# A stick-breaking attention whose pairs of heads share one score tile, and whose sample part is scanned

## The chip, the cores and the metric

The kernel runs on one core of one Trainium2 chip. The metric is device time in microseconds (us) of one execution, the median over runs. Five engines work beside each other, each with its own list of instructions taken strictly in order: TensorE (PE in the profile; its weight loads are PEld), VectorE (DVE), ScalarE (ACT), GpSimd (POOL) and SyncE (SP, which here issues DMAs).

## The reference, cut to what matters

One step of a two-layer encoder runs for 256 prompt frames and 32 sample frames together (`T = 288` columns). Layer 0 mixes frames with two softmax attentions (A and B), layer 1 with a stick-breaking attention (C). Cross-attention into 256 memory tokens and a squared-ReLU MLP follow in both layers. Only C is touched here. It has 16 heads of 64 features:

```python
def stick_breaking_attend(q, k, v, q_pos, k_pos):
    z = jnp.einsum('bqhd,bkhd->bhqk', q, k) * (HEAD_DIM ** -0.5)
    before = k_pos[None, :] < q_pos[:, None]
    log_keep = jnp.where(before, jax.nn.log_sigmoid(-z), 0.0)
    tail = lax.cumsum(log_keep, axis=3, reverse=True) - log_keep
    w = jnp.where(before, jnp.exp(jax.nn.log_sigmoid(z) + tail), 0.0)
    return jnp.einsum('bhqk,bkhd->bqhd', w, v)
```

The prompt's 256 queries see the prompt's 256 keys. The 32 sample queries see 256 cached keys and their own 32. With sp = softplus(z), the weight is exp(z minus the sum of sp over all keys from this one up to the query).

## The kernel before, in words

Activations lie with features on partitions and frames in columns. Every weight matrix streams in chunks of 256 columns. `load_chunk` lets SP load a raw fp32 chunk; ACT (and at times DVE) then rounds it into `wh`, a 4-byte type named fp32r that TensorE reads in one pass, and DVE or POOL subtracts to make the rest `wl`. `gemm2` makes each product from three matmuls (L159 to L161: high by high, low by high, high by low) into two PSUM banks named `g`, from a pool of three. The three `g` lines are most of the program.

Layer 1's attention is one phase, written in the order `ORD_C`: memory split, then for four groups of four heads `q` (queries and keys, `project_qk`), `p` (values, `project_v`) and `a` (`attend_c`), then `K0` to `K3`, the memory keys for the cross-attention that follows, and the output projection. That order is only a priority: the tile framework schedules all instructions against its own timeline and writes one fixed list for each engine. So PE's list has attention matmuls in between the `g` matmuls.

In `attend_c` each group has two pairs of heads (`p` = 0, 1); a pair shares one block of 128 feature rows, 64 for each head. Before the change it works as follows.

- Queries. `project_qk` writes them twice, each copy with the other head's 64 rows set to zero (`qz[:, p, par, :]`, by the mask `m8`), so that all 128 rows can be contracted.
- Scores of a pair. Keys lie on partitions. Bank `za` holds keys 0 to 127 against all queries of both heads (512 columns), bank `zb` keys 128 to 255 against queries 128 to 255 (256 columns). Queries and keys are split into fp32r halves (`split_into`), and three matmuls make each product (L578, L579).
- Softplus. ACT takes Abs (two calls), Exp and Ln, DVE finishes with max and add (two calls) into `sp`; POOL zeroes what is not below the diagonal (`below_diag`, two calls); ACT and DVE split `sp` into `sph` and `spl`.
- The running sum along keys is three matmuls for each of the halves, against a triangle of -1 (`mtrir`) and a block of -1 (`monesr`), added into `za` and `zb` (L599 to L601).
- Weights `w`: two Exp on ACT, two `below_diag` on POOL. `pv_prompt` (L473) multiplies with the values into `za`, `put_prompt` (ACT, then DVE) reads that out.
- The sample's scores `zs` also have keys on partitions: six plain fp32 matmuls (L618, L621), softplus in two pieces, five plain fp32 matmuls for the running sum (L628 to L632), two Exp, one select, `pv_sample` (L483), `put_sample`.

PSUM in this phase: three `g` banks, one bank `ps_t` for transposes and norms, and four banks for `za`, `zb` and `zs`. Plain fp32 matmuls stand in the trace as two passes each, so counts of their rows are double.

Of the kernel before, what the change touches and what calls it, by code (L numbers as in the profile page):

```python
# [52 lines left out]
def body(ctx: ExitStack, tc: tile.TileContext, i: dict, o: dict):  # L53
# [27 lines left out]
    def phase(kind):  # L81
        if R.stack is not None:
            R.stack.close()
        R.stack = ExitStack()
        R.step, R.pool_every, R.dve_every = STEP[kind]
        R.c = int(kind == "c")
        R.ph = R.stack.enter_context(tc.tile_pool(name="ph_" + kind, bufs=1))
        R.s = R.stack.enter_context(tc.tile_pool(name="s_" + kind, bufs=4 if kind[0] == "c" else 2, space=PS))
        R.m, R.o = ps_t, R.s
# [175 lines left out]
    fbias = const.tile([8, 1], F32, name="fbias")  # L265
    nc.sync.dma_start(out=fbias, in_=i["fbias"])
    eye32 = const.tile([P, NS], F32, name="eye32")
    for a in range(4):
        r = slice(32 * a, 32 * a + 32)
        dve.tensor_copy(eye32[r, :], ident[r, r])  # L270
        dve.tensor_copy(smask[r, NP_:T], bmask[r, P + 32 * a:P + 32 * a + 32])

    mtrir = const.tile([P, P], F32R, name="mtrir")
    dve.tensor_copy(mtrir, mtri_)
    mtri = mtrir.bitcast(F32)
    monesr = const.tile([P, P], F32R, name="monesr")
    dve.tensor_copy(monesr, mones_)
    mones = monesr.bitcast(F32)
# [3 lines left out]
    dve.tensor_copy(bdr, bd)  # L282

    qg = const.tile([P, 2, 2], F32, name="qg")
    for a in range(2):
# [100 lines left out]
        rstd_of(ps[:, 0:T], T, 1.0 / 64, r)  # L386

    def project_qk(wname, cq, ck, xh, xl, rs, norm, ko, oidx, ws0=None):
        qz = R.ph.tile([P, 2, 2, T], F32, tag="qz", name="qz", bufs=QZB[R.c])
        kT = R.ph.tile([P, 2, T], F32, tag="kT", name="kT", bufs=KTB[R.c])  # L390
        for which, chunk in ((0, cq), (1, ck)):
            ws = load_chunk(i[wname][chunk]) if ws0 is None or which else ws0
            pss = gemm2(ws, xh, xl, pool=R.s if FIRST_S and ws0 is not None and not which else ps_g)
            for p in range(2):
                ps = pss[p]
                if norm is None:
                    if which == 0:
# [140 lines left out]
        put_sample(oh, ol, kt0, po)  # L538


    def softplus(zs, w, a):

        c0 = 0
        for z in zs:
            c1 = c0 + z.shape[1]
            act(a[:, c0:c1], z, AF.Abs)
            c0 = c1
        act(a, a, AF.Exp, scale=-1.0)
        act(a, a, AF.Ln, bias=1.0)
        c0 = 0  # L550
        for z in zs:
            c1 = c0 + z.shape[1]
            dve.scalar_tensor_tensor(w[:, c0:c1], z, 0.0, a[:, c0:c1], ALU.max, ALU.add)
            c0 = c1

    def below_diag(x, pattern):

        nc.gpsimd.affine_select(x, x, pattern=pattern, compare_op=ALU.is_gt, fill=0.0, base=0,
                                channel_multiplier=-1)

    def attend_c(g, qz, kT, vt, ck, cv, oh, ol):
        kt0 = 2 * g
        k_ = dict(start=False, skip_group_check=True)
        for p in range(2):

            za = bank(R.s, "za")
            zb = bank(R.s, "zb")
            za2 = za.rearrange("p (e q) -> p e q", e=2)
            if ZR:
                qh = R.ph.tile([P, 2, NP_], F32R, tag="qh", name="qh")  # L570
                ql = R.ph.tile([P, 2, NP_], F32R, tag="ql", name="ql")
                kh = R.ph.tile([P, NP_], F32R, tag="kh", name="kh")
                kl = R.ph.tile([P, NP_], F32R, tag="kl", name="kl")
                split_into(kh, kl, kT[:, p, 0:NP_])
                split_into(qh, ql, qz[:, p, :, 0:NP_])
                f_ = True
                for x, y in ((kh, qh), (kh, ql), (kl, qh)):
                    mm(za2, x[:, 0:P], y, start=f_, stop=False, skip_group_check=True)  # L578
                    mm(zb[:, 0:NP_], x[:, P:NP_], y[:, :, P:NP_], start=f_, stop=False, skip_group_check=True)  # L579
                    f_ = False  # L580
            else:
                mm(za2, kT[:, p, 0:P], qz[:, p, :, 0:NP_], start=True, stop=False, skip_group_check=True)
                mm(zb[:, 0:NP_], kT[:, p, P:NP_], qz[:, p, :, P:NP_], start=True, stop=False, skip_group_check=True)
            a = R.ph.tile([P, 768], F32, tag="a", name="a", bufs=2)
            sp = R.ph.tile([P, 768], F32, tag="pr", name="sp", bufs=4)
            softplus([za, zb[:, 0:NP_]], sp, a)
            dia = [[0, 2], [1, P]]
            below_diag(sp[:, 0:512].rearrange("p (e q) -> p e q", e=2)[:, :, 0:P], dia)
            below_diag(sp[:, 512:768].rearrange("p (e q) -> p e q", e=2), dia)
            sh = R.ph.tile([P, 768], F32R, tag="a", name="sph", bufs=2)  # L590
            if SHE:
                dve.tensor_copy(sh, sp)
            else:
                act(sh, sp, AF.Copy)
            sl = R.ph.tile([P, 768], F32R, tag="pr", name="spl", bufs=4)
            dve.tensor_tensor(sl, sp, sh.bitcast(F32), ALU.subtract)
            for x, end in ((sh, False), (sl, True)):
                xb = x[:, 512:768]
# [3 lines left out]
            w = R.ph.tile([P, 768], F32, tag="pr", name="w", bufs=4)  # L602
            act(w[:, 0:512], za, AF.Exp)
            act(w[:, 512:768], zb[:, 0:NP_], AF.Exp)
            below_diag(w[:, 0:512].rearrange("p (e q) -> p e q", e=2)[:, :, 0:P], dia)
            below_diag(w[:, 512:768].rearrange("p (e q) -> p e q", e=2), dia)
            po = za
            pv_prompt(po, p, vt, [(w[:, par * NP_:(par + 1) * NP_], w[:, 512 + par * P:512 + (par + 1) * P])
                                  for par in range(2)])
            put_prompt(oh, ol, kt0 + p, po)  # L610

        z = bank(R.s, "zs")
        fl = True
        for p in range(2):
            q = qz[:, p, :, NP_:T]
            for kk in range(2):
                c0 = kk * P + p * 64
                mm(z[:, c0:c0 + 64], ck[:, p, kk * P:(kk + 1) * P], q, start=fl, stop=False, skip_group_check=True)  # L618
                fl = False
            c0 = 2 * P + p * 64  # L620
            mm(z[0:NS, c0:c0 + 64], kT[:, p, NP_:T], q, start=False, stop=False, skip_group_check=True)  # L621
        a = R.ph.tile([P, 768], F32, tag="a", name="as_", bufs=2)
        sp = R.ph.tile([P, 768], F32, tag="pr", name="sps", bufs=4)
        softplus([z[:, 0:2 * P]], sp[:, 0:2 * P], a[:, 0:2 * P])
        softplus([z[0:NS, 2 * P:384]], sp[0:NS, 2 * P:384], a[0:NS, 2 * P:384])
        n3 = sp[0:NS, 2 * P:384]
        below_diag(n3, [[0, 4], [1, NS]])
        mm(z[:, 0:2 * P], mtri, sp[:, 0:2 * P], stop=False, **k_)  # L628
        mm(z[:, 0:P], mones, sp[:, P:2 * P], stop=False, **k_)
        for c0 in (0, P):  # L630
            mm(z[:, c0:c0 + P], mones[0:NS, :], n3, stop=False, **k_)
# [5 lines left out]
        act(w3, z[0:NS, 2 * P:384], AF.Exp)
# [379 lines left out]
```

## Time and profile before

| | us |
|---|---|
| median of 3 runs | 972.64 (972.23 to 972.69) |
| the profiled execution | 970.67 |
| its span, first to last instruction | 969.0 |
| PE busy in it | 955.4 |
| DVE, ACT, POOL busy | 681.5, 541.6, 249.2 |

Between 500 and 672 us lies layer 1's C phase with its memory keys and its output projection. Durations of one matmul in the profile include a tail that overlaps with the next, so the time that a matmul costs in a stream is read from the distance between starts.

### The profile page before, as it was taken

Reading aid. Unit: us, or ns where it says so; the run is one execution under the profiler, and the core shown is the slowest. Engines: PE = TensorE matmul, PEld = TensorE weight load, DVE = VectorE, ACT = ScalarE, POOL = GpSimd, SP = SyncE. Lnnn points to the kernel's source line nnn. Section 1 sums busy time; section 2 is a strip of 40 time slices with the busy share of each in tenths; the row PEclk is TensorE's granted clock in tenths of the full one; section 3 lists DMA queues with packets and bytes.
Section 4 is the critical chain, followed back from the end, with each engine's and each line's share of the span. In section 5 each row is a group of like instructions: output and inputs, shape, how many; then the busy total and the mean of one; then the engine's idle time right before and its main releaser. Section 6 shows DMA issues by size and latency. Waiting matters only on the chain.

```text
span 969.0 us, 19373 instructions
## 1 busy us (share of the span) xinstructions
PE 955.4 (99%) x7276; PEld 922.2 (95%) x7276; DVE 681.5 (70%) x1460; ACT 541.6 (56%) x1268; POOL 249.2 (26%) x291
## 2 busy tenths in 40 slices
PE   8999989999999999999999999999999999999998
PEld 8998878999999999999999999989999999999998
DVE  8788848879678767776695656778977766464643
ACT  6667647656456645444474677865554655454531
POOL 4311472221212211121122322323543112121110
PEclk8999998999999999999999999999999999999999
DMA  8654353754555555555566444356443455555452
GB/s 264 200 173 162 116 198 112 245 167 141 170 170 171 161 168 166 162 170 163 168 197 207 142 142 152 100 196 200 139 157 127 153 175 169 162 167 169 160 174 72
DMA packets 50702, 160.03 MB, mean 165 GB/s; under 512 B 6296, under 2 KB 12968, under 8 KB 50352
## 3 DMA queue, kind: packets, MB, share of 16 engines
q1 hardware_dynamic: 46864, 148.69, 47.9%
q0 software_dynamic: 2592, 8.92, 2.4%
q10 hardware_dynamic: 1152, 1.18, 0.4%
q8 instruction: 57, 0.93, 0.4%
q14 instruction: 37, 0.30, 0.1%
HBM read 148.65 MB, written 10.12 MB: 164 GB/s over the span
## 4 chain that ended last, share of the span: by engine, by line
PE 91%; DMA 3%; DVE 3%; issue 2%; POOL 1%; ACT 0%; SPq 0%; DVEq 0%; ACTq 0%; POOLq 0%
PE g L159 27%; PE g L161 27%; PE g L160 26%; DVE wl L145 1%; DMA raw<-in_w_kv_dram 1%; DMA bsmp<-cd 1%; PE za L473 1%; PE za L578 1%; DMA b<-cd 1%; PE zs L618 0%; PE s L516 0%; POOL b L844 0%; PE sx L159 0%; PE po L473 0%; PE za L599 0%
## 5 line engine op out<-in xcount | busy, mean ns | idle before, releaser
L144 ACT ACTIVATE wh<-raw 128x512 fp32r<-128x512 f32 (+3 forms) x561 | 279.8, 550 | 234.2 <-PE g L160 116.3
L145 DVE TENSOR_TENSOR wl<-raw,wh 128x512 fp32r<-128x512 f32 (+3 forms) x483 | 315.7, 687 | 113.7 <-ACT wh L144 107.5
L145 POOL TENSOR_TENSOR wl<-raw,wh 128x512 fp32r<-128x512 f32 (+2 forms) x141 | 175.0, 1241 | 530.8 <-ACT wh L144 430.7
L159 PE MATMUL g<-xh,wh 128*128 128x288 f32 (+1 forms) x1032 | 303.1, 298 | 1.1 <-ACT wh L144 0.7
L161 PE MATMUL g<-xh,wl 128*128 128x288 f32 (+1 forms) x1032 | 302.9, 298 | 1.3 <-DVE wl L145 1.2
L160 PE MATMUL g<-xl,wh 128*128 128x288 f32 (+1 forms) x1032 | 303.8, 297 | 0.0
L161 PEld LDWEIGHTS g<-xh,wl 128*128 128x128 f32 (+1 forms) x1032 | 193.0, 188 | 4.0 <-DVE wl L145 2.6
L159 PEld LDWEIGHTS g<-xh,wh 128*128 128x128 f32 (+1 forms) x1032 | 192.5, 188 | 2.7 <-ACT wh L144 0.9
L160 PEld LDWEIGHTS g<-xl,wh 128*128 128x128 f32 (+1 forms) x1032 | 193.4, 188 | 0.9 <-DVE xl L197 0.2
L160 PE MATMUL g<-hl,wh 128*128 128x288 f32 x512 | 150.3, 295 | 0.0
L159 PE MATMUL g<-hh,wh 128*128 128x288 f32 x512 | 148.9, 295 | 0.0
L161 PE MATMUL g<-hh,wl 128*128 128x288 f32 x512 | 148.5, 294 | 0.0
L160 PEld LDWEIGHTS g<-hl,wh 128*128 128x128 f32 x512 | 96.1, 188 | 0.0
L161 PEld LDWEIGHTS g<-hh,wl 128*128 128x128 f32 x512 | 95.7, 188 | 0.0
L159 PEld LDWEIGHTS g<-hh,wh 128*128 128x128 f32 x512 | 95.3, 187 | 0.0
L160 PE MATMUL g<-ol,wh 128*128 128x288 f32 x256 | 75.0, 295 | 0.0
L161 PE MATMUL g<-oh,wl 128*128 128x288 f32 x256 | 74.3, 295 | 0.0
L159 PE MATMUL g<-oh,wh 128*128 128x288 f32 x256 | 73.7, 295 | 0.3 <-ACT oh L492 0.3
L774 DVE TENSOR_TENSOR h<-h,g 128x288 f32<-128x288 f32 x64 | 28.8, 449 | 29.6 <-PE g L161 29.5
L161 PEld LDWEIGHTS g<-oh,wl 128*128 128x128 f32 x256 | 47.9, 188 | 0.4 <-issue 0.4
L160 PEld LDWEIGHTS g<-ol,wh 128*128 128x128 f32 x256 | 48.0, 188 | 0.0
L764 ACT ACTIVATE squ<-tu 128x288 f32<-128x288 f32 x64 | 27.9, 437 | 35.8 <-DVE tu L762 35.7
(313 smaller groups left out, 1525.2 us busy)
## 6 DMA issues: line engine op xcount, KB each, us to landing
raw<-in_w_up_dram SPq DMA_DIRECT2D x64, 512.0 KB, 3.8
raw<-in_w_down_dram SPq DMA_DIRECT2D x64, 512.0 KB, 3.8
raw<-in_w_kv_dram SPq DMA_DIRECT2D x32, 512.0 KB, 4.0
raw<-in_sb_w_dram SPq DMA_DIRECT2D x24, 512.0 KB, 4.8
raw<-in_ab_w_dram SPq DMA_DIRECT2D x22, 512.0 KB, 4.8
raw<-in_w_q_dram SPq DMA_DIRECT2D x16, 512.0 KB, 4.6
raw<-in_w_o_dram SPq DMA_DIRECT2D x16, 512.0 KB, 4.0
raw<-in_ab_wo_dram SPq DMA_DIRECT2D x8, 512.0 KB, 4.9
```

The lines of the kernel that those rows point to most:

```text
L144: act(wh[:, r, :], src, AF.Copy)
L145: e.tensor_tensor(wl[:, r, :], src, wh[:, r, :].bitcast(F32), ALU.subtract)
L159: mm(out, lh, rh, start=first, stop=False)
L160: mm(out, lh, rl, start=False, stop=False)
L161: return mm(out, ll, rh, start=False, stop=last)
L473: mm(po[64 * par:64 * par + 64, kk * P:NP_], vt[:, kk, cols], pts[par][kk], start=kk == 0, stop=kk == 1)
L578: mm(za2, x[:, 0:P], y, start=f_, stop=False, skip_group_check=True)
L764: act(sq, t, AF.Square)
L774: dve.tensor_tensor(h[:, kt, :], h[:, kt, :], ps[:, 0:T], ALU.add)
```

## The change: what it does

- Queries are not padded: `qz` is one copy, scaled by 0.125.
- A pair's scores lie in one tile `zz` of two banks, one bank for each head, 384 columns in each: three blocks of 128 queries (two for keys 0 to 127, one for keys 128 to 255), ordered so that the four blocks on the diagonal are neighbours. The matmuls are plain fp32, four of them, each contracting only the 64 rows of its head: one head sits in array rows 0 to 63, the other in 64 to 127. The fp32r split of queries and keys is gone.
- Every elementwise step of a pair is one instruction over 768 columns: one Abs, one max-add, one select, one Exp.
- The running sum has a matmul of 384 columns and one of 128 columns for each head and each half.
- The sample has queries on partitions (two heads of 32 queries for each `p`, 128 rows in all), keys along columns. ACT makes padded queries for the 32 sample columns only; four plain fp32 matmuls give scores; DVE scans them from the last key backwards; three transposes on PE bring the weights back to keys on partitions. This part is written ahead of the pairs, its end behind the first pair.
- PSUM: `zz` has two buffers of two banks. The sample's `zs`, `ps_ws` (the transposes) and `pos` now take turns in the single bank `ps_t`, with the transposes of the values and the norms.
- At the start DVE makes three small constants more (`below`, `notbelow`, `m01`).

```diff
-        qz = R.ph.tile([P, 2, 2, T], F32, tag="qz", name="qz", bufs=QZB[R.c])
+        qz = R.ph.tile([P, 2, T] if norm is None else [P, 2, 2, T], F32, tag="qz", name="qz", bufs=QZB[R.c])
...
-                        for par in range(2):
-                            dve.scalar_tensor_tensor(qz[:, p, par, :], ps[:, 0:T], m8[:, par:par + 1], rs,
-                                                     ALU.mult, ALU.mult)
+                        dve.scalar_tensor_tensor(qz[:, p, :], ps[:, 0:T], 0.125, rs, ALU.mult, ALU.mult)
...
-        R.s = R.stack.enter_context(tc.tile_pool(name="s_" + kind, bufs=4 if kind[0] == "c" else 2, space=PS))
+        R.s = R.stack.enter_context(tc.tile_pool(name="s_" + kind, bufs=2, space=PS))
...
+    def block(x, e, kk):
+        b = x[:, e, 0:384].rearrange("p (b c) -> p b c", b=3)
+        return (b[:, 1::-1, :] if kk == 0 else b[:, 2:3, :]) if e == 0 else (b[:, 0:3:2, :] if kk == 0 else b[:, 1:2, :])
...
+        for par in range(2):
+            act(qs[:, :, par, :], qz[:, :, NP_:T], AF.Copy, scale=m01[:, par:par + 1])
+        zp = bank(ps_t, "zs")
+        for p in range(2):
+            dst = zp[64 * p:64 * p + 64, :]
+            q = qs[:, p, :, :]
+            mm(dst[:, 0:NP_], q, ck[:, p, :], start=True, stop=True)
+            mm(dst[:, NP_:T], q, kT[:, p, NP_:T], start=True, stop=True)
...
+        dve.tensor_copy(z, zp[:, 0:T])
+        softplus(z, sp, su)
+        dve.tensor_tensor(sp[:, NP_:T], sp[:, NP_:T], below, ALU.mult)
+        dve.tensor_tensor_scan(su[:, ::-1], sp[:, ::-1], sp[:, ::-1], 0.0, ALU.add, ALU.max)
+        dve.tensor_tensor(w[:, 0:T], z, su, ALU.subtract)
+        dve.tensor_tensor(w[:, NP_:T], w[:, NP_:T], notbelow, ALU.add)
+        act(w[:, 0:T], w[:, 0:T], AF.Exp)
...
+            zz = R.s.tile([P, 2, 512], F32, tag="zz", name="zz")
+            for kk in range(2):
+                for e in range(2):
+                    r = slice(64 * e, 64 * e + 64)
+                    mm(block(zz, e, kk), kT[r, p, kk * P:(kk + 1) * P], qz[r, p, kk * P:NP_].rearrange("p (b c) -> p b c", c=P),
+                       start=kk == 0, stop=False, skip_group_check=True)
+            softplus(zv, sp, a)
+            below_diag(sp)
+            act(sh, sp, AF.Copy)
             dve.tensor_tensor(sl, sp, sh.bitcast(F32), ALU.subtract)
             for x, end in ((sh, False), (sl, True)):
-                mm(za, mtrir, x[:, 0:512], stop=False, **k_)
-                mm(za2[:, :, P:NP_], monesr, xb.rearrange("p (e q) -> p e q", e=2), stop=end, **k_)
-                mm(zb[:, 0:NP_], mtrir, xb, stop=end, **k_)
+                for e in range(2):
+                    mm(zz[:, e, 0:384], mtrir, x[:, e, :], stop=False, **k_)
+                    mm(block(zz, e, 0)[:, 1, :], monesr, block(x, e, 1)[:, 0, :], stop=end, **k_)
+            act(w_, zv, AF.Exp)
+            below_diag(w_)
...
+            if p == 0:
+                pp = bank(ps_t, "ps_ws")
+                for kk in range(3):
+                    nc.tensor.transpose(pp[:, kk * P:(kk + 1) * P], w[:, kk * P:(kk + 1) * P], ident)
+                act(pt[:, 0:384], pp[:, 0:384], AF.Copy)
+                po = bank(ps_t, "pos")
```

The lists of all engines are the same in both kernels outside the C phase, but for the three constants and a few swaps in the phases after it. Within it they are rescheduled. Rows read: line, operation, output <- inputs with the number of each buffer, shape.

PE before, the scores of the third group's first pair and what comes next:

```order
L578 MATMUL za_7781<-qh_7783,kh_7785 128x512
L579 MATMUL zb_7782<-qh_7783,kh_7785 128x256
L578 MATMUL za_7781<-ql_7784,kh_7785 128x512
L579 MATMUL zb_7782<-ql_7784,kh_7785 128x256
L578 MATMUL za_7781<-qh_7783,kl_7786 128x512
L579 MATMUL zb_7782<-qh_7783,kl_7786 128x256
L159 MATMUL g_7936<-xh_6601,wh_7922 128x288
```

PE after, the same pair, now `zz_7748`:

```order
L607 MATMUL zz_7748<-qz_7165,kT_7166 128x2x128 x2
L607 MATMUL zz_7748<-qz_7165,kT_7166 128x128
L438 MATMUL ps_vt_7709<-ident_117,vT_7639 128x128 x2
L439 MATMUL ps_vt_7709<-ident_117,vT_7639 32x128
L607 MATMUL zz_7748<-qz_7165,kT_7166 128x128
L157 MATMUL g_8048<-mh_6669,wh_8041 128x256
```

Six wide matmuls over all array rows became four on half the rows; here, and in two other pairs, three transposes of the values were scheduled in between.

PE before, the last group's first pair, the last rows ahead of its product with the values and that product (`zs` is the sample's, `g_8434` and `g_8435` belong to the memory keys K3). Ahead of this piece, behind the pair's last running-sum matmul, stand 19 more `g` rows:

```order
L160 MATMUL g_8435<-ml_6660,wh_8419 128x256
L161 MATMUL g_8435<-mh_6659,wl_8420 128x256
L159 MATMUL g_8434<-mh_6659,wh_8419 128x256
L618 MATMUL zs_8099<-qz_7552,ck_8001 128x64
L473 MATMUL za_8005<-w_8041,vt_7918 64x256 x2
L618 MATMUL zs_8099<-qz_7552,ck_8001 128x64
L473 MATMUL za_8005<-w_8041,vt_7918 64x128 x2
```

PE after, the same pair (`zz_7944`) from its last running-sum matmul on, and the last pair (`zz_7998`):

```order
L619 MATMUL zz_7944<-spl_7957,monesr_250 128x128
L488 MATMUL pos_7983<-wts_7981,cv_7921 64x32 x8
L488 MATMUL pos_7983<-wts_7981,vt_7836 64x32 x4
L478 MATMUL zz_7944<-w_7968,vt_7836 64x256 x2
L478 MATMUL zz_7944<-w_7968,vt_7836 64x128 x2
L335 MATMUL ps_xn_8101<-sh_8107,onesr_252 128x256
L336 MATMUL ps_xn_8101<-sl_8109,onesr_252 128x256
L618 MATMUL zz_7998<-sph_8010,mtrir_248 128x384
L619 MATMUL zz_7998<-sph_8010,monesr_250 128x128
L618 MATMUL zz_7998<-sph_8010,mtrir_248 128x384
L619 MATMUL zz_7998<-sph_8010,monesr_250 128x128
L335 MATMUL ps_xn_8193<-sh_8199,onesr_252 128x256
```

The `g` rows that stood between the running sum and the product with the values are gone from this place, and the last pair's running sum has moved up to right behind it. The scores of `zz_7998` stand only seven running-sum matmuls (of `zz_7944`) and three transposes ahead of this piece.

ACT after, the same stretch:

```order
L614 ACTIVATE sph_7956<-sp_7950 128x768
L596 ACTIVATE sps_7933<-sps_7933 128x288
L631 ACTIVATE wts_7981<-ps_ws_7977 128x384
L548 ACTIVATE a_8003<-zz_7998 128x768
L621 ACTIVATE w_7968<-zz_7944 128x768
L549 ACTIVATE a_8003<-a_8003 128x768
L497 ACTIVATE oh1_6667<-pos_7983 128x2x32
L550 ACTIVATE a_8003<-a_8003 128x768
L492 ACTIVATE oh1_6667<-zz_7944 128x256
L181 ACTIVATE rx_8113<-ps_xn_8101,epsb_105 128x256
L343 ACTIVATE sqx_8194<-tmk_8139 128x256
```

ACT before, around the same pair (`za_8005`, `zb_8006`):

```order
L594 ACTIVATE sph_8031<-sp_8022 128x768
L546 ACTIVATE a_8068<-za_8052 128x512
L492 ACTIVATE oh1_6657<-zs_7875 128x2x32
L144 ACTIVATE wh_8427<-raw_8425 128x512 x2
L603 ACTIVATE w_8041<-za_8005 128x512
L604 ACTIVATE w_8041<-zb_8006 128x256
L546 ACTIVATE a_8068<-zb_8053 128x256
L183 ACTIVATE rx_8315<-ps_xn_8303,epsb_105 128x256
```

What moved: the next pair's Abs (`a_8003`) now stands whole ahead of this pair's Exp (`w_7968`), and the next pair's Exp and Ln follow at once, with no weight split (`wh`) between.

More of the change, by code (lines that the diff above doesn't have):

```diff
@@ L87, in phase @@
         R.ph = R.stack.enter_context(tc.tile_pool(name="ph_" + kind, bufs=1))
-        R.s = R.stack.enter_context(tc.tile_pool(name="s_" + kind, bufs=4 if kind[0] == "c" else 2, space=PS))
-        R.m, R.o = ps_t, R.s
+        R.s = R.stack.enter_context(tc.tile_pool(name="s_" + kind, bufs=2, space=PS))
+        R.m = ps_t
         if kind[0] != "c":
@@ L267, in body @@
     eye32 = const.tile([P, NS], F32, name="eye32")
+    below = const.tile([P, NS], F32, name="below")
     for a in range(4):
@@ L270, in body @@
         dve.tensor_copy(eye32[r, :], ident[r, r])
+        dve.tensor_scalar(below[r, :], mtri_[r, r], -1.0, None, ALU.mult)
         dve.tensor_copy(smask[r, NP_:T], bmask[r, P + 32 * a:P + 32 * a + 32])
+    dve.tensor_tensor(below, below, eye32, ALU.subtract)
+    notbelow = const.tile([P, NS], F32, name="notbelow")
+    dve.tensor_scalar(notbelow, below, 1.0, -NEG, ALU.subtract, ALU.mult)
     mtrir = const.tile([P, P], F32R, name="mtrir")
     dve.tensor_copy(mtrir, mtri_)
-    mtri = mtrir.bitcast(F32)
     monesr = const.tile([P, P], F32R, name="monesr")
     dve.tensor_copy(monesr, mones_)
-    mones = monesr.bitcast(F32)
     onesr = const.tile([P, P], F32R, name="onesr")
@@ L282, in body @@
     dve.tensor_copy(bdr, bd)
+    m01 = const.tile([P, 2], F32, name="m01")
+    dve.tensor_scalar(m01, m8, 8.0, None, ALU.mult)
     qg = const.tile([P, 2, 2], F32, name="qg")
@@ L538, in attend_ab, with softplus, below_diag @@
         put_sample(oh, ol, kt0, po)
[L541 to L547, printed above, removed]
+    def softplus(z, sp, a):
+        act(a, z, AF.Abs)
         act(a, a, AF.Exp, scale=-1.0)
         act(a, a, AF.Ln, bias=1.0)
[L550 to L558, printed above, removed]
+        dve.scalar_tensor_tensor(sp, z, 0.0, a, ALU.max, ALU.add)
+    def below_diag(x):
+        v = x.rearrange("p e c -> p (e c)")[:, P:5 * P].rearrange("p (b c) -> p b c", b=4)
+        nc.gpsimd.affine_select(v, v, pattern=[[0, 4], [1, P]], compare_op=ALU.is_gt, fill=0.0, base=0,
                                 channel_multiplier=-1)
@@ L563, in attend_c @@
         k_ = dict(start=False, skip_group_check=True)
-        for p in range(2):
[L566 to L595, printed above, removed]
@@ new lines, in attend_c @@
+        dve.tensor_copy(z, zp[:, 0:T])
+        spt = tile_p("sps").rearrange("p e c -> p (e c)")
+        sp, w = spt[:, 0:T], spt[:, 384:768]
+        softplus(z, sp, su)
+        dve.tensor_tensor(sp[:, NP_:T], sp[:, NP_:T], below, ALU.mult)
+        dve.tensor_tensor_scan(su[:, ::-1], sp[:, ::-1], sp[:, ::-1], 0.0, ALU.add, ALU.max)
+        nc.gpsimd.memset(w[:, T:384], 0.0)
+        dve.tensor_tensor(w[:, 0:T], z, su, ALU.subtract)
+        dve.tensor_tensor(w[:, NP_:T], w[:, NP_:T], notbelow, ALU.add)
@@ new lines, in attend_c @@
+        act(w[:, 0:T], w[:, 0:T], AF.Exp)
[6 more added lines that the diff above has]
+                       start=kk == 0, stop=False, skip_group_check=True)
+            zv = zz[:, :, 0:384]
+            a, sp = tile_a("a"), tile_p("sp")
+            softplus(zv, sp, a)
+            below_diag(sp)
+            sh, sl = tile_a("sph", F32R), tile_p("spl", F32R)
+            act(sh, sp, AF.Copy)
@@ L605, in attend_c @@
[L605 to L609, printed above, removed]
-            put_prompt(oh, ol, kt0 + p, po)
[L612 to L631, printed above, removed]
@@ new lines, in attend_c @@
+            w_ = tile_p("w")
+            act(w_, zv, AF.Exp)
+            below_diag(w_)
+            po = zz[:, 0, :]
+            pv_prompt(po, p, vt, [(block(w_, e, 0), block(w_, e, 1)) for e in range(2)])
+            put_prompt(oh, ol, kt0 + p, po)
+            if p == 0:
+                pp = bank(ps_t, "ps_ws")
+                for kk in range(3):
+                    nc.tensor.transpose(pp[:, kk * P:(kk + 1) * P], w[:, kk * P:(kk + 1) * P], ident)
+                pt = tile_a("wts").rearrange("p e c -> p (e c)")
+                act(pt[:, 0:384], pp[:, 0:384], AF.Copy)
+                po = bank(ps_t, "pos")
+                pv_sample(po, cv, vt, [pt[:, 0:P], pt[:, P:2 * P], pt[:, 2 * P:384]], lambda p, par: (2 * p + par) * NS)
+                put_sample(oh, ol, kt0, po)
```

23 lines of the change are left out of this document (7 added, 16 removed).

## The prediction

> **What bounds the kernel now.** I read the page's busy shares and the chain that ended last first, then a table by stretches of time, then PE's timeline inside the C phase. The page:
>
> ```profile
> PE 955.4 (99%) x7276; PEld 922.2 (95%) x7276; DVE 681.5 (70%) x1460; ACT 541.6 (56%) x1268; POOL 249.2 (26%) x291
> PE 91%; DMA 3%; DVE 3%; issue 2%; POOL 1%; ACT 0%; SPq 0%; DVEq 0%; ACTq 0%; POOLq 0%
> ```
>
> TensorE is busy 99% of the span and holds 91% of the chain. The C phase is no exception. In the table by stretches (length, then busy time of PE, PEld, DVE, ACT, POOL, then PE's granted clock):
>
> ```profile
> 500.00:672.00 172.00, 171.06 (x1341) 160.71 (x1341) 116.54 (x213) 112.84 (x247) 50.67 (x77) 1.00 0.50 164
> ```
>
> PE stands idle for 0.94 us of 172. DVE and ACT have a third of the time free. So the change is worth what it takes from PE's list, less what PE then waits in it; elementwise work saved beside PE is worth nothing by itself. PE's waits here are one place, the sample of the last group:
>
> ```profile
> 646.68 0.66 PE L483 MATMUL zs<-ws,cv 128*64 128x32 f32 x16 [0.62 <-ACT ws L637]
> ```
>
> There nothing but attention work stood in PE's list, and it waited for ACT's Exp. I take this row as the model of what a crowded place costs.
>
> **The change part by part: PE's work.** Prices are distances between starts. A stretch of PE's timeline with the old forms (start, duration, line, operation):
>
> ```profile
> 553.95 0.87 PE L473 MATMUL za<-w,vt 128*64 128x256 f32 x8
> 554.75 0.38 PE L579 MATMUL zb<-qh,kh 128*128 128x256 f32 x1
> 554.97 0.40 PE L578 MATMUL za<-ql,kh 128*128 128x512 f32 x1
> 555.20 0.28 PE L579 MATMUL zb<-ql,kh 128*128 128x256 f32 x1
> 555.32 0.59 PE L628 MATMUL zs<-sps,mtrir 128*128 128x256 f32 x2
> 555.75 0.39 PE L629 MATMUL zs<-sps,monesr 128*128 128x128 f32 x2
> 556.07 0.71 PE L631 MATMUL zs<-sps,monesr 32*128 32x128 f32 x4
> 557.03 0.50 PE L578 MATMUL za<-qh,kl 128*128 128x512 f32 x1
> ```
>
> The reader is to see five prices. An fp32r matmul of 512 columns takes 0.23 (554.97 to 555.20), one of 256 takes 0.12. A plain fp32 one of 256 takes 0.43 (555.32 to 555.75), so 128 columns take 0.215. L473's four products take 0.80 (553.95 to 554.75); by 0.43 and 0.215 they would take 1.29 one after another, so the two heads, in different array columns, run together. And a change of the array's shape costs about 0.2: behind L473 a 256-column matmul takes 0.22 instead of 0.12 (0.10, its weights are not loaded ahead), and ahead of L631, which uses 32 rows, L629 takes 0.32 instead of 0.215 (0.10 until the array is empty).
>
> Scores of a pair. Removed: 3 x (0.23 + 0.12) = 1.05. Added: 0.43 + 0.215 = 0.65 if the two heads' row halves run together as L473's column halves do, and a shape change in and out, 0.4: 1.05 as well. No row shows two row halves; one after another they would cost 1.29 + 0.4 = 1.69. I take the first, by the nearest row (L473). In three pairs the order puts transposes between the four, 0.4 more each, and one pair follows another directly, 0.4 less: +0.8 in all.
>
> Running sum of a pair. Removed: 2 x (0.23 + 0.12 + 0.12) = 0.94. Added: four of 384 columns, 0.175 each between those rows, and four fp32r of 128. No row shows an fp32r matmul under 256 columns. Below, half of 0.12 is 0.06; above, the plain fp32 price, 0.215. Each has new weights of 128 columns, whose late load was 0.10 above; so I take 0.11. 4 x 0.285 = 1.14: +0.20 a pair, 1.6 for eight; bounds 0 and 5.0.
>
> The Trainium skill ("TensorE: Matmul & The Clock Gate", section "Back-to-back issue gap") gives about 81 ns per matmul for a stream of loads and 128-column matmuls; 32 of them at that price instead of 0.11 would make the sum 0.9 us less. No row here shows it.
>
> Products with the values (L473, L483) keep count and shape; where the order now sets products of one shape side by side, changes of shape fall away, six times 0.2: -1.2.
>
> Sample of a group. Removed: its scores and its running sum (555.32 to 557.03, 1.71). The scores of one group, around an L473:
>
> ```profile
> 545.13 0.55 PE L618 MATMUL zs<-qz,ck 128*128 128x64 f32 x4
> 546.21 0.87 PE L473 MATMUL za<-w,vt 128*64 128x256 f32 x8
> 547.01 0.43 PE L618 MATMUL zs<-qz,ck 128*128 128x64 f32 x2
> 547.60 0.40 PE L160 MATMUL g<-xl,wh 128*128 128x288 f32 x1
> ```
>
> 1.08 + 0.59 = 1.67, and 0.1 for the `g` behind: 3.48 in all. Added are four matmuls in the very form that layer 0 has, and three transposes, also there:
>
> ```profile
> 53.05 0.66 PE L505 MATMUL ss<-ck,qs 128*64 128x256 f32 x4
> 53.72 0.70 PE L516 MATMUL s<-kT,qz 128*128 128x256 f32 x2
> 170.78 0.55 PE L533 MATMUL ps_pts<-ident,prs 128*128 128x128 f32 x3
> 171.09 0.36 PE L331 MATMUL ps_xn<-sl,onesr 128*128 128x256 f32 x1
> ```
>
> 0.67 with 0.2 for the shape, and 0.31: 1.18. So -2.3 a group, -9.2 for four.
>
> PE's work: -9.2 + 0.8 + 1.6 - 1.2 = -8.0 us.
>
> **The waits it adds.** The order decides these. All pairs but two keep 19 to 31 `g` rows (2.5 to 4 us) between `spl` and the product with the values. The first pairs of groups 3 and 4 have none, and behind a waiting product stand all later rows of PE; ACT's `put_prompt` waits with it and holds the weight splits that follow in its list. Durations, from ACT, DVE and POOL by shape in the C phase (busy, mean ns of one):
>
> ```profile
> L548 ACT ACTIVATE a<-a 128x768 f32<-128x768 f32 x8 | 6.7, 840 | 0.0
> L594 ACT ACTIVATE sph<-sp 128x768 fp32r<-128x768 f32 x8 | 6.7, 832 | 1.8 <-POOL sp L558 1.8
> L487 ACT ACTIVATE oh<-za 128x256 fp32r<-128x256 f32 x8 | 3.1, 385 | 4.9 <-PE za L473 4.9
> L435 ACT ACTIVATE vt<-ps_vt 128x256 f32<-128x256 f32 x8 | 3.0, 381 | 0.2
> L596 DVE TENSOR_TENSOR spl<-sp,sph 128x768 fp32r<-128x768 f32 x8 | 8.1, 1008 | 2.1 <-ACT sph L594 2.1
> L488 DVE TENSOR_TENSOR ol<-za,oh 128x256 fp32r<-128x256 f32 x8 | 3.3, 416 | 0.9 <-ACT oh L487 0.9
> L558 POOL TENSOR_SCALAR_AFFINE_SELECT w<-w 128x256 f32<-128x256 f32 x16 | 7.8, 507 | 8.0 <-ACT w L603 8.0
> ```
>
> An instruction over 768 columns costs 0.84, a select over 512 I put at 0.8, between one of these and two.
>
> Group 3, first pair. Behind `spl` PE has only the sample's products (0.8) until `w` is there. ACT owes the copy of the transposed weights and the next pair's Abs (over 1 us together, partly begun) ahead of Exp (0.84), then POOL the select (0.8): PE waits 1.5. Next come the values' transposes, twice through the one bank `ps_t`; the second set waits for ACT's `put_prompt` (0.39) and two copies of the first (0.38 and some 0.25): 0.95. Together 2.4.
>
> Group 4. The last pair's scores take the buffer of the pair whose product ended just before: they wait for ACT (0.39) and DVE (0.42) of `put_prompt` and the product's own tail, 1.2. The first pair's product waits as in group 3, 1.5, and 0.2 for `spl`. Then the last pair's `sph` stands in PE's list, and its chain has only begun: from the start of its Abs run Abs, the other pair's Exp, Exp and Ln on ACT (about 0.8 each), DVE's max-add (1.0, as L596), the select (0.8) and ACT's copy (0.84), with hand-overs 6.1 in all, against 3.7 that PE has to do or waits for already: 2.4. `spl` follows 1.0 behind `sph`, which covers 0.6, with DVE late: 0.8. Together 6.1. Without any queueing, by bare chains, the two places cost 1.7 and 3.8. No `g` can fill in: the fixed list has none, and the next ones need a PSUM bank that DVE frees behind these very steps. So 8.5, bounds 5.5 and 9.3; and the old 0.9 falls away, since the last group's sample is no longer at the end.
>
> A gap also touches the clock. Around the old kernel's largest gap:
>
> ```profile
> 137.10:140.50 3.40, 2.75 (x19) 1.42 (x15) 0.68 (x2) 1.37 (x3) 0.46 (x1) 1.00 0.95 330
> 140.50:143.90 3.40, 1.52 (x29) 1.09 (x27) 0.65 (x2) 1.10 (x3) 3.40 (x4) 1.00 0.37 148
> 143.90:150.70 6.80, 5.18 (x16) 4.10 (x17) 3.85 (x22) 3.77 (x15) 2.01 (x3) 0.50 0.00 0
> 144.95 1.22 PE L317 MATMUL ps_ms<-mssum,ones 128*128 128x256 f32 x2 [2.29 <-POOL mssum L314]
> ```
>
> After 3.4 us with PE 1.52 busy the clock stood at half for 6.8 us; with 2.75 busy it did not. In group 4 PE does about 1.8 us of work in 6.7, so I expect one such step. Of the 6.8 us about 3 are waiting anyway; half of the rest is 1.9. Bounds 0 and 6.8 (a second step in group 3, none of it hidden).
>
> The Trainium skill's rule ("TensorE: Matmul & The Clock Gate", section "HAM oscillation — how this bites in real kernels") is that PE keeps its clock as long as no idle gap exceeds about 3.4 us. Here the trace differs: its step came with a longest gap of 2.29 us. By the rule there would be no step, since no gap worked out above exceeds 2.5.
>
> **The rest.** The three constants stand ahead of DVE's first split of the input:
>
> ```profile
> 3.88 0.52 DVE L197 SCALAR_TENSOR_TENSOR xl<-h,gT,xh 128x288 fp32r<-128x288 f32 x1 [0.19 <-ACT xh L196]
> 5.40 1.95 DVE L145 TENSOR_TENSOR wl<-raw,wh 128x256 fp32r<-128x256 f32 x1 [1.00 <-ACT wh L144]
> ```
>
> Seven small instructions, some 0.2 each, against 1.0 of idle time: +0.2 (bounds 0 and 0.5). ACT loses 16 splits and 20 calls by merging, POOL 24 selects, DVE 8 query copies, 16 splits and 8 calls by merging, and gains four small steps a group. All of that lies beside PE's `g` rows, and where it does not it is in the chains above. SP issues the same loads, POOL the same stores.
>
> Sum: -8.0 + 8.5 - 0.9 + 0.2 + 1.9 = +1.7 us on 970.67, the profiled execution (969.0 of span and 1.7 around it). The median of the runs is 1.97 above that one, so the forecast is 972.64 + 1.7 = 974.3: no change that can be told, leaning to slower.
>
> **The rivals.**
> - The clock stays full: -0.2, 972.4. For it: the gap of 0.62 at 646 cost no clock. Against: the row at 140.50. This is how the Trainium skill's rule above would have it.
> - The waits fill up, since the other engines run ahead: 3 us of waits instead of 8.5 and no clock step, -5.7, 966.9. For it: ACT and DVE have a third of the time free, and bare chains are already 3 us less. Against: each link above is a buffer or a value, not speed. It decides from 7 us of waits down.
> - Short fp32r matmuls cost the plain price: 32 x 0.105 = +3.4, 977.7. For it: no row shows one. Against: width alone has never changed the price per column from 512 to 256.
> - The row halves run one after another: 8 x 0.64 = +5.1, 979.4. For it: the only row-split matmul (L631) runs alone. Against: L473 and L505 overlap in columns.
>
> **How the numbers follow.** Forecast 0.36, clock full 0.10, waits filled 0.23, short matmuls 0.21, row halves 0.10. 0.2% is 1.9 us, about what a measurement of this kernel can tell from no change. Faster: the filled waits, 0.23. Slower: the last two and a third of the forecast, 0.43. Same: the rest, 0.34. The range, 967.0 to 979.5, reaches from the filled waits to the row halves and leaves out half of each; the forecast's own, by the bounds of waits and clock, is 970 to 978.
>
> **What would show it.** Right: PE busy in the C phase down by 8, waits of 1 to 2.5 us ahead of L478 and L618 in its last third, and a stretch at clock 0.50 behind them. The 128-column matmuls of L619 should start the next 0.11 later, and L607's two heads within 0.02 of each other. Wrong: L619 at 0.2, heads 0.4 apart, or no waits at L478, which would mean that my chains are too long.

## The result and the profile after

The changed kernel takes 980.06 us (median of 4 runs, 978.22 to 982.75), the kernel before 972.43 beside it: a ratio of 1.0076, interval 1.0048 to 1.0105. The forecast was 974.3, slower by 1.7; it is slower by 7.6. The profiled execution took 979.83 (span 978.0). All ratios below are of runs in the usual state: one of the six runs of the pairs alone took 3767.68 and is left out of its ratio. First the page's busy shares and its chain, then the table by stretches for 500 to 673 us (columns as before):

```profile
PE 954.4 (98%) x7264; PEld 922.1 (94%) x7264; DVE 677.9 (69%) x1451; ACT 535.0 (55%) x1232; POOL 241.6 (25%) x267
PE 89%; DVE 3%; DMA 3%; issue 1%; POOL 1%; ACT 1%; SPq 0%; DVEq 0%; ACTq 0%; POOLq 0%
500.00:673.00 173.00, 164.64 (x1289) 154.35 (x1288) 105.82 (x188) 103.84 (x207) 40.06 (x49) 0.96 0.48 157
```

PE now stands idle for 8.4 us of the C phase instead of 0.94, and its clock there is 0.96 instead of 1.00. The waits of PE in it (total, times, longest):

```profile
PE zz L478 <- POOL w L556: 2.6, 2, 1.3
PE zz L618 <- ACT sph L614: 2.2, 1, 2.2
PE ps_ws L629 <- ACT sps L596: 1.7, 2, 1.3
PE zz L607 <- DVE ol L493: 0.9, 1, 0.9
PE ps_vt L438 <- ACT vt L441: 0.6, 1, 0.6
PE zz L618 <- DVE spl L615: 0.2, 1, 0.2
```

All lie in groups 3 and 4. PE's timeline in group 3, first pair:

```profile
605.79 0.92 PE L607 MATMUL zz<-qz,kT 64*128 64x256 f32 x8
606.64 0.38 PE L159 MATMUL g<-mh,wl 128*128 128x256 f32 x1
...
610.79 0.33 PE L618 MATMUL zz<-sph,mtrir 128*128 128x384 f32 x1
610.96 0.22 PE L619 MATMUL zz<-sph,monesr 128*128 128x128 f32 x1
611.02 0.39 PE L618 MATMUL zz<-sph,mtrir 128*128 128x384 f32 x1
611.25 0.22 PE L619 MATMUL zz<-sph,monesr 128*128 128x128 f32 x1
612.81 0.55 PE L629 MATMUL ps_ws<-ident,sps 128*128 128x128 f32 x3 [1.34 <-ACT sps L596]
...
616.11 1.55 PE L478 MATMUL zz<-w,vt 128*64 128x256 f32 x8 [1.28 <-POOL w L556]
...
621.90 0.41 PE L158 MATMUL g<-ml,wh 128*128 128x256 f32 x1
622.12 0.41 PE L159 MATMUL g<-mh,wl 128*128 128x256 f32 x1
```

The reader sees the two prices that were in dispute: a pair's scores take 0.85 (605.79 to 606.64, where one head after the other was put at 1.29 and more), so the two row halves run together, and a 128-column fp32r matmul takes 0.06 (610.96 to 611.02), with 0.17 and 0.23 for the 384-column ones around it. Then come two waits of 1.3 us, and behind them a 256-column `g` matmul takes 0.22 (621.90 to 622.12) instead of 0.12: the granted clock is at half (0.50 below). The same stretch in pieces of 3.41 us, cut where the clock changes (length, PE busy, then the other engines; the clock is the third number from the end):

```profile
608.70:612.12 3.42, 2.77 (x23) 2.56 (x22) 3.35 (x4) 1.32 (x2) 2.25 (x2) 1.00 0.20 73
612.12:615.53 3.41, 2.02 (x31) 1.68 (x31) 1.03 (x2) 2.58 (x5) 0.11 (x1) 1.00 0.45 144
615.53:618.94 3.41, 2.38 (x11) 1.19 (x11) 1.60 (x3) 2.15 (x6) 1.28 (x3) 0.50 0.00 0
618.94:622.36 3.42, 3.25 (x15) 2.44 (x16) 1.71 (x3) 1.38 (x4) 0.00 (x0) 0.50 0.00 0
622.36:625.77 3.41, 3.41 (x19) 2.80 (x18) 0.69 (x1) 1.50 (x3) 0.00 (x0) 0.50 0.03 5
625.77:629.18 3.41, 3.41 (x29) 3.37 (x27) 1.06 (x2) 3.10 (x6) 0.41 (x1) 1.00 0.29 84
...
636.01:639.43 3.42, 2.14 (x37) 1.57 (x35) 0.24 (x2) 3.37 (x6) 0.64 (x1) 1.00 0.00 0
639.43:642.84 3.41, 1.20 (x9) 0.99 (x7) 3.06 (x7) 3.04 (x7) 0.90 (x2) 1.00 0.00 0
642.84:646.25 3.41, 3.17 (x15) 2.88 (x14) 2.11 (x5) 0.91 (x2) 0.82 (x2) 0.50 0.22 82
```

Two stretches at half, of three pieces and of one, 13.65 us in all, each behind a piece in which PE did little (2.02 and 1.20).

**Where the time went.** Both lists of PE hold the same `g` matmuls outside the phase, so the two traces can be laid over each other. The changed one is later by 1.51 us at 20 us, by 2.56 at 160, by 2.59 at 520, and by 9.02 from 665 on. Between one `g` matmul ahead of the phase and one behind it, each line's matmuls at full clock (start to next start), the waits, and the rest, which is what half clock added (an estimate, since it rests on the full-clock price of each line), in us:

| | before | changed | only pairs | only sample |
|---|---|---|---|---|
| length | 180.00 | 186.43 | 188.57 | 181.06 |
| scores of pairs | 9.25 | 8.31 | 8.08 | 8.80 |
| running sum of pairs | 7.62 | 9.60 | 9.07 | 7.97 |
| sample, without products | 13.70 | 3.92 | 13.12 | 3.89 |
| products with the values | 10.22 | 9.38 | 9.76 | 10.75 |
| g, transposes, norms | 138.25 | 141.05 | 141.65 | 139.80 |
| PE's work in all | 179.04 | 172.25 | 181.68 | 171.21 |
| waits | 0.95 | 8.4 | 4.8 | 7.7 |
| added by half clock | 0 | 5.8 | 2.1 | 2.1 |

The last two columns are runs told below. So in the C phase: work -6.8, waits +7.5, clock +5.8, together +6.4. A second estimate of the clock agrees: 12.2 us of work were done at half clock, and at 0.213 for 0.119, the distances of the `g` matmuls at half and at full clock, that adds 5.4. With 1.5 at the start the parts make 7.9, near the 7.6 of the medians. The two profiled executions are 9.2 apart (979.83 and 970.67). The 1.05 that they lose between 20 and 160 us, under the same list of PE, I don't count: the traces below without the constants at the start lose -0.1 to 2.2 there against the kernel before, and the profiled execution before was 1.8 under the median of its runs.

### The profile page after: what moved, and what is told of

Read it like the earlier page. It is cut to its first block, busy times and chain, and to the rows that moved or that the text cites. A ratio compares the mean times of both kernels' runs of the same rounds, so it can differ in the third digit from the quotient of the medians.

```text
span 978.0 us, 19276 instructions
## 1 busy us (share of the span) xinstructions
PE 954.4 (98%) x7264; PEld 922.1 (94%) x7264; DVE 677.9 (69%) x1451; ACT 535.0 (55%) x1232; POOL 241.6 (25%) x267
## 4 chain that ended last, share of the span: by engine, by line
PE 89%; DVE 3%; DMA 3%; issue 1%; POOL 1%; ACT 1%; SPq 0%; DVEq 0%; ACTq 0%; POOLq 0%
PE g L157 27%; PE g L159 26%; PE g L158 26%; DVE wl L143 1%; DMA raw<-in_w_kv_dram 1%; DMA bsmp<-cd 1%; PE zz L607 1%; PE zz L478 1%; PE zz L618 1%; DMA b<-cd 1%; PE s L521 0%; DMA raw<-in_ab_w_dram 0%; PE sx L157 0%; PE po L478 0%; PE ps_vt L438 0%
```

## The experiments

Theory: the start lost 1.5 us to the constants; in the C phase the sample's new form is a gain on PE, the pairs' new form a small loss, and both are outweighed by crowded places, which cost twice, as waits and as clock. Rivals: the start is chance; the pairs' long steps make the waits, whatever the order; the clock matters little.

**The constants made later.** The edit (the three constants are made when the phase begins, `below` from `mtrir`):

```diff
-        dve.tensor_scalar(below[r, :], mtri_[r, r], -1.0, None, ALU.mult)
...
     phase("c")
+    held_c = tc.issue_after(last_dve[0].ins)
+    held_c.__enter__()
+    below = const.tile([P, NS], F32, name="below")
...
```

> The changed kernel, with the three constants made when the C phase begins instead of at the start; all else on every engine stands in the same order. Theory A (DVE's constants ahead of its first split of the input are what the start lost): the 1.50 us by which the two traces are apart 18 us into the program go, and with them the 1.07 us by which they drift further apart up to 155 us, which I put down to a clock step that falls on other work: 1.5 to 2.6 us less than the changed kernel, 977.5 to 978.6 if the kernel before is at 972.4. In the C phase the waits (about 8.5 us) and a clock step remain. Rival B (the constants are hidden, as the prediction had it, and the start differs by chance): no change, 980.0.

Measured: 978.85 (974.45 to 985.23, 12 runs), ratio to before 1.0064 (1.0043 to 1.0085); again, in a later session, 977.70 and 1.0062 (1.0040 to 1.0085), each within 0.3 us of its expected range.

> The kernel with late constants once more, beside the next one on the same chip, since its times spread widely. All theories: 978 to 980, ahead of group 3's product about 1.3 us of waiting twice, and a slow stretch behind.

**The constants added to the kernel before.**

```diff
+        dve.tensor_scalar(below[r, :], mtri_[r, r], -1.0, None, ALU.mult)
...
+    dve.tensor_tensor(below, below, eye32, ALU.subtract)
+    dve.tensor_scalar(notbelow, below, 1.0, -NEG, ALU.subtract, ALU.mult)
+    dve.tensor_scalar(m01, m8, 8.0, None, ALU.mult)
```

> The kernel before, with the three constants made at the start as in the changed kernel (seven small DVE instructions that nothing reads); all else in the same order. Theory A: 1.5 to 2.6 us slower than the kernel before, 974.0 to 975.0. Rival B: 0.2 us, 972.6.

Measured: 973.91, ratio 1.0016 (0.9999 to 1.0032), so +1.6 us with an interval of -0.1 to +3.1. The times of these runs alone would not settle it. The traces do: at 20 us this kernel is 2.68 behind the kernel before, and the changed kernel with late constants is 1.61 ahead of the changed one. Of the ten traces without the constants at the start, nine lie within 0.4 of the kernel before there; one, with two pieces at half clock at 9 us, is 1.14 behind. DVE's timeline at the start, of the changed kernel, then POOL's and PE's:

```profile
3.12 3.90 DVE L271 TENSOR_SCALAR below<-mtri 32x32 f32<-32x32 f32 x4
...
7.68 0.52 DVE L195 SCALAR_TENSOR_TENSOR xl<-h,gT,xh 128x288 fp32r<-128x288 f32 x1
5.69 1.28 POOL L207 TENSOR_TENSOR sq<-h 128x288 f32<-128x288 f32 x2
8.26 0.85 PE L158 MATMUL g<-xl,wh 128*128 128x288 f32 x2 [2.39 <-DVE xl L195]
```

Then DVE with late constants, and DVE of the kernel before with constants added:

```profile
3.84 0.52 DVE L196 SCALAR_TENSOR_TENSOR xl<-h,gT,xh 128x288 fp32r<-128x288 f32 x1
5.27 2.17 DVE L143 TENSOR_TENSOR wl<-raw,wh 128x256 fp32r<-128x256 f32 x1 [0.92 <-ACT wh L142]
```

```profile
2.95 0.83 DVE L272 TENSOR_SCALAR below<-mtri 32x32 f32<-32x32 f32 x4
...
4.87 2.48 DVE L275 TENSOR_TENSOR below<-below,eye 128x32 f32<-128x32 f32 x1
...
7.52 0.52 DVE L197 SCALAR_TENSOR_TENSOR xl<-h,gT,xh 128x288 fp32r<-128x288 f32 x1
```

In every one of these traces the DVE instruction that runs when POOL squares its inputs ends only at 7.0 to 7.4, less than 0.3 behind POOL (6.97 to 7.30). Without the constants that is `wl`, and `xl` is long done (4.4). With them it is a constant, and `xl` comes behind, at 8.2. So the price is not their seven times 0.2 but the place they take: `xl` now stands behind the instruction that ends late. Theory A holds; its size is 1.5 to 2.7 us in the traces.

**One part of the change alone.** The pairs' form with the old sample (whose bank is `ps_t`), and the sample's form with the old pairs:

```diff
# only pairs: the old sample, padded queries from qs
-        zp = bank(ps_t, "zs")
...
+        z = bank(ps_t, "zs")
+            q = qs[:, p, :, :]
...
# only sample: the kernel before, with the new sample's lines
+        zp = bank(ps_t, "zs")
...
+                pp = bank(ps_t, "ps_ws")
...
+                po = bank(ps_t, "pos")
```

> Only the pairs of heads in the new form; the sample in the old one, with keys on partitions, written behind the pairs and in the bank ps_t. The start as in the kernel before. By the prediction's terms for PE's work: scores +0.8, running sum +1.6, shapes -1.2, so +1.2 us. In PE's list 18 to 32 g rows stand between spl and the product with the values in every pair, so theory C (the waits come from the sample's three uses of the single bank ps_t ahead of the products, not from the pairs' form) expects waits of only 1.5 to 3 us, at the end of the last group: 974.0 to 976.5. Rival D (the pairs' wide steps themselves are too long a chain): waits of 7 us or more and a clock step, 980 or more.

> Only the sample in the new form (queries on partitions, scan, transposes, in the bank ps_t); the pairs as before, with their padded fp32r queries. Constants made when the C phase begins. By the prediction's term PE's work falls by 9.2 us. In PE's list two places are crowded, the second pair of the third group (no g row between spl and the product) and the end of the last group; at 1.5 to 2.5 us each, with the old wait of 0.9 gone, theory C gives 966 to 968, up to 970 with a clock step. Rival E (the sample's new form is not 2.3 us a group cheaper on PE): 972 or more.

Measured: pairs alone 980.73, ratio 1.0073 (1.0048 to 1.0097); sample alone 973.81, ratio 1.0011 (0.9997 to 1.0026). Both missed what theory C gave, upwards, and reached the times that rivals D and E gave. But PE's work in the sample alone is 7.8 less than before, so rival E falls (9.2 were expected), and rival D is tested below. Their waits, pairs alone first, then sample alone (line numbers are each kernel's own):

```profile
PE ps_xn L331 <- DVE sh L328: 2.7, 1, 2.7
PE g L158 <- DVE h L644: 0.9, 1, 0.9
```

```profile
PE ps_xn L331 <- DVE sh L328: 2.7, 1, 2.7
PE ps_ws L637 <- ACT sps L585: 2.0, 1, 2.0
```

Both wait longest, or nearly so, in the same place, which neither the pairs nor the sample has of its own: the norms of the memory keys (`ps_xn`). They too take the bank `ps_t`, in program order, so K0's norm can't begin before the last group's sample has left it, and K1's follows it. With the sample alone, K0's norm starts 0.06 behind DVE's read of the sample's result (`ol`, done at 633.15), and K1's waits behind it:

```profile
633.21 0.58 PE L331 MATMUL ps_xn<-sh,onesr 128*128 128x256 f32 x1 [0.58 <-DVE ol L494]
636.73 0.55 PE L331 MATMUL ps_xn<-sh,onesr 128*128 128x256 f32 x1 [2.72 <-DVE sh L328]
```

PE takes its list in order, so the `g` matmuls behind these norms, which could fill it, are held too. In the kernel before the sample took a bank of the scores' pool. Theory C fell in its form, and became J: it is the order in which one bank is handed out.

**The bank.** The sample alone again, with its transposes and products in a bank of the scores' pool; and with another order of parts:

```diff
-                pp = bank(ps_t, "ps_ws")
+                pp = bank(R.s, "ps_ws")
...
-                po = bank(ps_t, "pos")
+                po = pp[:, 384:512]
```

> The sample alone in the new form (as in the run of that part), but its transposes and its products go to a bank of the pool of the scores instead of ps_t. Theory J (with the sample in ps_t the norms of the memory keys K0 and K1 have to wait for the last sample, since ps_t is handed out in program order, and with them the g banks): the 7.7 us of waits fall to 2 to 4 us, the half clock to at most 1.5 us; with PE's work at 171.2 us against 179.0 this gives 966 to 969, faster than the kernel before. Rival K (the waits come from the sample's own long chain at the end): 972 or more.

> The same with the order 'M q0 p0 a0 q1 p1 a1 q2 p2 a2 K0 q3 p3 a3 K1 K2 K3'. In PE's list only the last pair's product stands without g rows ahead of it. Theory J: waits of 2 to 3 us, 965.5 to 968.5. Rival K: 972 or more.

Measured: 966.43 and 966.43, ratios 0.9944 (0.9925 to 0.9963) and 0.9938 (0.9925 to 0.9951): faster than the kernel before by 0.6%, and 7 us faster than with the sample in `ps_t`. The waits of the first of them:

```profile
PE za L474 <- POOL w L559: 1.0, 1, 1.0
PE g L160 <- ACT oh L488: 0.5, 1, 0.5
```

7.7 us of waits became 1.6, and the phase is 5.8 us shorter than before; rival K falls. The whole phase is scheduled anew by this edit, so it shows that the crowd goes with the bank, not which single wait did. In the whole change those four banks are the two buffers of `zz`, so this edit has no run there.

**The pairs alone, with K0 and K1 ahead of the last attention group.**

```diff
-ORD_C = 'M q0 q1 p0 a0 q2 p1 a1 q3 p2 a2 p3 a3 K0 K1 K2 K3'.split()
+ORD_C = 'M q0 q1 p0 a0 q2 p1 a1 q3 p2 a2 p3 K0 K1 a3 K2 K3'.split()
```

> Only the pairs in the new form, the old sample in ps_t, with K0 and K1 written ahead of the last attention group, so that their norms take ps_t before that group's sample. Theory J: the 4.8 us of waits at the end of that run and its slow stretch go (waits under 1.5 us), and what stays is the pairs' own work, +2.6 us by the sums of that trace: 974 to 976. Rival D (the pairs' chain is too long): waits of 4 us or more, 979 to 981.

Measured: 975.02, ratio 1.0034 (1.0022 to 1.0047), with these waits:

```profile
PE g L158 <- DVE tmk L353: 0.5, 1, 0.5
PE g L158 <- ACT oh L493: 0.3, 1, 0.3
PE ps_xn L331 <- ACT sph L594: 0.3, 1, 0.3
```

4.8 us became 1.1, no half clock is left in the phase, and up to 740 us it has lost 2.4 us against the kernel before. So the pairs' chain is not too long (rival D falls), and what is left is their price on PE: the pairs' new form alone loses some 2.5 us.

**The whole change in another order.**

```diff
+ORD_C = 'M q0 p0 a0 q1 p1 a1 q2 p2 a2 K0 q3 p3 a3 K1 K2 K3'.split()
```

> The changed kernel with late constants and another order of the phase's parts: 'M q0 p0 a0 q1 p1 a1 q2 p2 a2 K0 q3 p3 a3 K1 K2 K3'. In PE's list only one product (the last group's first pair) stands without g rows ahead of it, against two, and the last pair's sph has a chunk ahead of it. The work is the same. Theory F (what the change loses is crowded places: 8.4 us of waits and 5.5 us of half clock behind them): waits of 3 to 5 us and one clock step of 1 to 3 us, so 5 to 8 us less than with late constants alone (978.85): 971 to 974. Rival G (the waits move to other places with the order): 977 or more.

Measured: 972.83, ratio 1.0007 (0.9996 to 1.0018), 6 us less than with late constants alone, as theory F had it. The waits:

```profile
PE zz L612 <- DVE spl L609: 2.0, 1, 2.0
PE zz L612 <- ACT sph L608: 1.0, 1, 1.0
PE pos L482 <- ACT wts L625: 0.6, 1, 0.6
```

The same work with 3.9 us of waits instead of 8.4: up to 740 us the phase has lost 0.2 us against the kernel before, not 6.4. One stretch of three pieces at half clock remains, more than theory F allowed for.

**Filling the waits.** Matmuls that nothing reads, in groups 3 and 4:

```diff
+                if g > 1 and p == 0 and not end:
+                    for n in range(16):
+                        mm(zz[:, n % 2, 384:512], mtrir, x[:, n % 2, 0:P], stop=False, **k_)
...
+                    for n in range(16):
+                        mm(po[:, P:2 * P], mtrir, onesr, stop=False, **k_)
```

> The changed kernel with late constants, and matmuls that nothing reads at the crowded places of groups 3 and 4: 16 fp32r ones of 128 columns behind the running sum of sph into unused columns of zz, 16 behind the sample's products into unused columns of pos, and in the last pair 7 plain ones behind its max-add. They add no waiting for other engines, but keep PE busy; some parts are scheduled elsewhere around them. Theory H (half of what the C phase lost is TensorE's clock, which drops after a stretch of about 3.4 us with less than some 2.1 us of work): at least one of the two slow stretches of the C phase goes, the waits shrink by what the matmuls fill, and the time falls by 2 to 5 us from 978.85, to 974 to 977, though work is added. Rival I (the waits alone cost, the clock little): no gain, 979 to 981.

Measured: 987.77, ratio 1.0154 (1.0129 to 1.0178). The time went the other way from theory H, and above rival I too. The run tests neither, since the list changed around the added matmuls (a new wait of 2.87 ahead of the fourth group's `sph`). In group 4 they ran at half clock, 3.08 us for 16 instead of 1.95:

```profile
608.44 1.95 PE L619 MATMUL zz<-sph,mtrir 128*128 128x128 f32 x16
...
631.01 3.08 PE L619 MATMUL zz<-sph,mtrir 128*128 128x128 f32 x16
```

With six and six instead of sixteen, and in group 3 alone, the lists of the attention stay as they are:

> Late constants, and in the third group alone twelve matmuls that nothing reads, in two waits of about 1.3 us: six fp32r ones of 128 columns (0.11 each in a row) behind the running sum of sph, six behind the sample's products. Up to the end of the attention all lists stand as without them. Theory H (a grid window of 3.41 us with less than about 2.1 us of work halves the clock): the window ahead of group 3's slow stretch then holds about 0.7 us more work than its 2.0, the stretch of 10.2 us (three windows) does not come, and with it go about 4 us, though no wait ends earlier: 973.5 to 976. Rival I (the clock's fall has other causes, or costs little beside the waits): no change, 978 to 980.

Measured: 978.02, ratio 1.0069 (1.0053 to 1.0085), beside 977.70 without them in the same session: no gain, so the times go with rival I. The traces say more. The pieces of 3.41 us ahead of and at the place of group 3's stretch, without the filling and with it:

```profile
610.65:614.06 3.41, 2.06 (x33) 1.68 (x31) 1.70 (x4) 1.83 (x4) 0.00 (x0) 1.00 0.48 154
614.06:617.47 3.41, 2.13 (x13) 1.20 (x11) 1.26 (x3) 2.49 (x5) 0.88 (x2) 0.50 0.00 0
```

```profile
609.53:612.94 3.41, 2.73 (x35) 2.35 (x33) 2.03 (x4) 1.50 (x3) 0.00 (x0) 1.00 0.50 154
612.94:616.35 3.41, 2.54 (x31) 1.76 (x27) 1.17 (x3) 3.19 (x8) 0.64 (x1) 1.00 0.00 0
```

With 2.73 of work instead of 2.06 the clock stayed up, as theory H says, and the phase of this execution is 2.8 us shorter. (The second pair of pieces lies 0.17 us ahead of its execution's own grid; on the grid they hold 2.73 and 2.37.) But over six runs each the mean time at half clock is the same (24.1 us with the filling, 23.1 without). In the profiled executions the stretch of group 4 is one piece long once and four pieces twice; whether that swing hides the gain is not settled.

What the clock costs can also be read from the runs. Eighteen runs of one kernel, the one with late constants, differ from 974.45 to 985.23, and their mean granted clock gives each one's time at half: the time rises by 0.41 us for each us at half clock (correlation 0.82). Over 57 runs of the kernel before the slope is 0.28. They spend 24.4 and 11.7 us at half on average. So 12.7 us more at half is 5.2 us at 0.41 and 3.6 at 0.28, an estimate that takes the slope for a cause. With the 5.4 to 5.8 of the trace it speaks against rival I's cheap clock. The filling did not show it, and no run took the half clock away and left all else as it was.

## Why the prediction was wrong

- **Waits (+8.5, old ones -0.9): right in sum, in part by luck.** 7.5 measured against 7.6. The places named waited, but each less than forecast, 6.5 in all: L478 twice at 1.3 (forecast 1.5 each), the second set of values' transposes 0.6 (0.95), the scores of the last pair 0.9 (1.2), its `sph` 2.2 (2.4), `spl` 0.2 (0.8). The transposes of the sample's weights (L629, 1.7) weren't named, and made up for the rest.
- **PE's work (-8.0): right in sign, 1.2 too much.** The sample gave 9.8 instead of 9.2 by its own lines. The running sum came near (2.0 more, forecast 1.6); the products gave 0.84 instead of 1.2. The scores' own lines fell by 0.94, where the forecast had +0.8 with the changes of shape around them; `g`, transposes and norms, in which such changes show, grew by 2.8. The pairs' form alone was forecast at +1.2 and costs 2.5.
- **The clock (+1.9): the first step that failed.** It took one stretch of 6.8 us in group 4, half of it hidden under waits. There were 13.65 us, in groups 3 and 4, with only 1.4 us of waiting in them: 5.8, within the forecast's bound of 6.8. Group 4's stretch was one piece, and cost about 1.4; group 3's was three and cost about 4.0 (estimates, from 3.2 and 9.0 us of work at 0.213 for 0.119). For group 3 the sum put nothing, though its upper bound named a step there. The piece ahead of that stretch holds 1.4 us of waiting, 0.7 of it at L629, which was not named, and 0.7 at L478; without the first it would have held some 2.7 of work, at which the clock stayed up elsewhere (run with six and six). The waits were forecast one by one and never added up over such a piece. The old kernel's step was read by its gap of 2.29, too, but only 1.24 of that lies ahead of the step at 143.90; what the step followed is a piece with 1.52 of work.
- **The start (+0.2): the second step that failed.** 1.5 measured. Durations of small instructions were summed against idle time. What was not asked is what stands behind them: the first split of the input moved from ahead of POOL's squares to behind them. The row that told it was quoted: `wl` at 5.40 took 1.95 there, and 0.41 to 1.0 later on.
- **The rivals.** Clock stays full: wrong, two steps with no gap over 2.3 us. Waits fill up: wrong. Short matmuls at the plain price: wrong, 0.06 between wide ones. Row halves one after another: wrong, 0.85 for a pair's scores. What happened was none of them, but the forecast's own mechanism with three terms mis-sized, the clock by 3.9, the start by 1.3 and PE's work by 1.2, and the waits by -0.1: 1.7 + 3.9 + 1.3 + 1.2 - 0.1 = 8.0 against 7.6.

## What to carry to other kernels

A pool with one buffer is a queue in program order: giving it one more user puts everything that comes later in the program behind that user, here the norms that free the fillers of TensorE, and that decided between 974 and 966 us with the same work. Gaps on TensorE can be paid twice, once as waits and again as clock on the work behind them, so in a kernel like this one waits should be added up over pieces of 3.4 us and not one by one. Before small instructions are put at the start of a queue, look for the instruction that will now come late, and at what it will then meet.

## What the runs showed of the hardware

All changes of the granted clock in one execution lie on one grid of 3.413 us: every stretch at half is one to four pieces long. Over the 13 traces, without the last 7 us of each, of the pieces at full clock in which PE's records cover up to 2.13 us 36 of 40 were followed by half clock, of the more than 50 with 2.14 to 2.9 none. The Trainium skill ("TensorE: Matmul & The Clock Gate", section "What's actually happening") says that the activity window is free-running and 3413 ns long; the traces agree. The same section lets the clock fall after an idle window; here 2.02 us of work in it did not keep it up. The four exceptions (1.59 to 2.03) stay unexplained.

DVE instructions beside POOL's squares took long: of the four 32x32 ones (3.90 us together) the last took 2.17, one of 128x32 took 2.48, and both ended 0.05 behind POOL's. The Trainium skill ("SBUF — State Buffer", section "Who interferes with whom") says that DVE and GpSimd share one port pair under an exclusive lock, that a DVE instruction with two SBUF inputs contends with a GpSimd instruction that reads SBUF, and that `tensor_scalar` can contend too. The traces fit that, but no run here took POOL's work away.

Sixteen fp32r matmuls of 128 columns in a row took 0.11 us each (608.44 to 610.23), though one between wide ones takes 0.06.
